# Where the softmax sums are divided out: spread by TensorE over the heads' outputs, or multiplied into the exponentials on ScalarE

## The chip, the core and the metric

The kernel runs on one core of a Trainium2 chip. Its metric is the device time of one execution in microseconds (us), median of three runs. Five engines take their instructions each from a queue of its own and in order: TensorE (PE, with its weight loads listed apart as PEld), VectorE (DVE), ScalarE (ACT), GpSimd (POOL) and SyncE (SP, which issues most DMAs). They meet at semaphores.

## The reference

A trunk of two layers over 512 frames of width 1024. Layer 0 has latent attention with 8 heads of 128 value features, layer 1 chunked attention with 16 heads of 64 features and a relative bias. A SwiGLU block follows each. What matters here is the softmax of both mixers:

```python
p = jax.nn.softmax(s, axis=-1).astype(v.dtype)        # layer 0
return jnp.einsum('bhqk,bkhd->bqhd', p, v)
...
p = jax.nn.softmax(s, axis=-1).astype(v_band.dtype)   # layer 1
o = jnp.einsum('bnhqk,bnkhd->bnqhd', p, v_band).reshape(B, S, B_HEADS * B_HEAD_DIM)
```

Each row of exponentials has to be divided by its sum. That can be done to the exponentials before the product with v, or to the product.

## The kernel before

All products are in fp32 split into a high and a low part, so that a product takes two or three passes of TensorE. `split` makes the parts: ACT casts the high one (L141), DVE subtracts it for the low one (L142).

A head is worked off in four slots, one for each block `qt` of 128 queries. Slot `qt` has `n = 128 * (qt + 1)` keys, so its tiles are 128, 256, 384 and 512 wide. `Head.scores` computes the scores on PE into a bank `sc` (L889 to L893 in layer 0, L1181 and L1182 in layer 1), then DVE adds mask or bias, takes the row minimum and writes the tile `p` (L396), and ACT makes the exponentials in place and adds up each row into one column of `sums` (L398, with a short second instruction that reads the accumulator). `Head.turn` has PE transpose `p` in blocks of 128x128 into a bank `pt` (L410), and splits the bank into `pth` and `ptl`. `pv` multiplies these with the values (L258 to L260 in layer 0, L1189 and L1190 in layer 1).

The products come out with features on the partitions and queries along the row, but `sums` has queries on the partitions. So the reciprocals have to be spread. In layer 0, `pv` takes the reciprocals of a head's four columns on DVE (L903), ACT copies the product out of its bank into `of` (L905), `spread` has PE transpose each column, broadcast to 128x128, into a bank `bc` (four transposes, L371), and DVE multiplies `of` by it (L908). In layer 1 two heads share the tile `of`: once for such a pair DVE takes the reciprocals (L1198), ACT writes them out as a tile `rw` in two copies (L1201), PE transposes that in four blocks into a bank `rs` (L1210), and DVE multiplies (L1211). Either way `of` is then split into `oh` and `ol`, the operands of the output projection.

`attention` runs the slots. While slot i is scored, slot i - 2 is turned; a head's `pv` follows six slots after its first. Between them `weave` puts steps of a filler: the projections of later heads, which need split weights (`whi`, `wlo`), and in the end the first output projections. The order on every engine is fixed when the program is built, by a list scheduler that goes by priorities and its own estimates of durations; on the chip each engine then keeps to that order. Banks are few: two for scores (tag `s`), two for transposes (tag `t`), four for products.

Of the kernel before, what the change touches and what calls it, by code (L numbers as in the profile page):

```python
# [11 lines left out]
F32R = mybir.dt.float32r  # L12
I32 = mybir.dt.int32
AF = mybir.ActivationFunctionType
OP = mybir.AluOpType
# [3 lines left out]
D, S, P = 1024, 512, 128  # L19
# [4 lines left out]
H_B, HD = 16, 64  # L24
# [6 lines left out]
NQT = S // P  # L31
# [37 lines left out]
def trunk(ctx: ExitStack, tc: tile.TileContext, a, out):  # L69
    nc = tc.nc  # L70
    V = nc.vector
# [10 lines left out]
    def name_(n):  # L82
        uid[0] += 1
        return f"{n}_{uid[0]}"

    def U(dt=F32, name="u"):
        return up.tile([P, S], dt, tag="u", name=name_(name), bufs=NU)
# [4 lines left out]
    def bank(tag="mm", name="b"):  # L92
        return ps.tile([P, S], F32, tag=tag, name=name_(name), bufs={"mm": 4, "s": 2, "t": 2}[tag])

    def small(name="sm"):
        return sp.tile([P, 4], F32, tag="small", name=name_(name))
# [17 lines left out]
    ident = consts.tile([P, P], F32, name="ident")  # L114
# [25 lines left out]
    def split(dst_hi, dst_lo, src):  # L140
        return (nc.scalar.copy(dst_hi, src),  # L141
                V.tensor_tensor(dst_lo, src, dst_hi.bitcast(F32), op=OP.subtract))  # L142
# [119 lines left out]
    def proj(n_out, n_k, kc, rhs, banks, ahead=True):  # L262

        cols = n_out * P
        for c in range(0, n_k, kc):
            m = min(kc, n_k - c)
            w = feed.next(m * cols, ahead)
            for kk in range(m):
                if kk == 1:
                    feed.ahead()  # L270
                while len(rhs) <= c + kk:
                    yield False
                for j in range(n_out):
                    mm3(banks[j], w(kk * cols + j * P, P), rhs[c + kk], c + kk == 0, c + kk == n_k - 1)
                    yield True
# [91 lines left out]
    def spread(col, first=0):  # L367

        b = bank("t", "bc")
        for i in range(col.shape[1]):  # L370
            nc.tensor.transpose(b[:, (first + i) * P:(first + i + 1) * P],  # L371
                                col[:, i:i + 1].to_broadcast([P, P]), ident)
        return b
# [8 lines left out]
    class Head:  # L382
# [7 lines left out]
        def scores(self, qt):  # L390
# [8 lines left out]
                                 accum_out=self.sums[:, qt:qt + 1])  # L399
            self.p[qt] = p  # L400

        def turn(self, qt):
            if self.pt is None:
                self.pt = [pool[0].tile([P, NQT, S], F32R, tag=t, name=name_(t), bufs=n)
                           for t, n in (("pth", 2), ("ptl", 1))]
            n = P * (qt + 1)
            p = self.p.pop(qt)
            t = bank("t", "pt")
            for kt in range(qt + 1):
                nc.tensor.transpose(t[:, kt * P:(kt + 1) * P], p[:, kt * P:(kt + 1) * P], ident)  # L410
            tv = t[:, :n].rearrange("p (a b) -> p a b", b=P)
            q_ = slice(qt * P, (qt + 1) * P)
            split(self.pt[0][:, :qt + 1, q_], self.pt[1][:, :qt + 1, q_], tv)

    def attention(n_heads, start, fill, first, units, after):


        slots = n_heads * NQT
        heads, done, late = {}, [0], []
        rate = (units - first) / slots  # L420

        def weave(upto):
            n = 0
            while (n < 4 if fill.scored else done[0] < upto) and fill.step():
                done[0] += 1
                n += 1

        for i in range(slots + 3):
            h, qt = divmod(i, NQT)
            if h < n_heads:  # L430
                if qt == 0:
                    heads[h] = start(h)
                    if h == 0:
                        weave(first)
                heads[h].scores(qt)
                fill.scored = i == slots - 1
            weave(first + rate * (i + 0.5))
            if late and not after:
                late.pop()()
            if i >= 6 and i % NQT == 2:  # L440
                t = heads.pop((i - 6) // NQT)
                late.append(t.pv(*t.pt))
            if 2 <= i < slots + 2:
                t, qt = divmod(i - 2, NQT)
                heads[t].turn(qt)
            if late and i % NQT == 3:
                late.pop()()
            weave(first + rate * (i + 1))
        if late:
            late.pop()()  # L450
# [231 lines left out]
    rest = proj(3, KT, 2, xs, b2)  # L682
# [4 lines left out]
    for j in range(2):  # L687
        t = U(name="ckv")
# [79 lines left out]
    qr, qk_a, osp = {}, {}, []  # L768
# [113 lines left out]
    def start_a(h):  # L882
        fill.until(h)
        qh, ql, kh, kl = qk_a.pop(h)
        r = qr.pop(h)

        def qk(o, qt, n):
            q_ = slice(qt * P, (qt + 1) * P)
            nc.tensor.matmul(o, qh[:, q_], kh[:, :n], start=True, stop=False)  # L889
            nc.tensor.matmul(o, qh[:, q_], kl[:, :n], start=False, stop=False)  # L890
            nc.tensor.matmul(o, ql[:, q_], kh[:, :n], start=False, stop=False)
            nc.tensor.matmul(o, r[:, q_], kr1[:, :n], start=False, stop=False)
            nc.tensor.matmul(o, r[:, q_], kr2[:, :n], start=False, stop=True)  # L893

        def pv(pth, ptl):
            fill.until("v")
            o = bank()
            v_ = slice(h * VD, (h + 1) * VD)
            for kt in range(NQT):
                q_ = slice(kt * P, S)  # L900
                mm3(o[:, q_], (va[kt][:, 0, v_], va[kt][:, 1, v_]), (pth[:, kt, q_], ptl[:, kt, q_]),
                    kt == 0, kt == NQT - 1)
            V.reciprocal(sums, sums)  # L903
            of = U(name="of")
            nc.scalar.copy(of, o)  # L905

            def rest():
                V.tensor_tensor(of, of, spread(sums), op=OP.mult)  # L908
                oh, ol = U(F32R, "oh"), U(F32R, "ol")
                split(oh, ol, of)  # L910
                osp.append((oh, ol))

            return rest

        sums = small("sums")
        return Head(qk, lambda n: mask[:, S - n:], lambda qt: nsq[:, qt:qt + 1], pv, sums)

    firsts = []
# [201 lines left out]
    rest = v_half(0)  # L1120
# [13 lines left out]
    osp, qk_b, ofs, sums, biases = [], {}, {}, {}, {}  # L1134
# [34 lines left out]
    def start_b(h):  # L1169
        pr, e = divmod(h, 2)  # L1170
        fill.until(pr)
        q1, k1, k2 = qk_b[pr]
        bt = biases.pop(h)
        if h + 1 < H_B:
            bias(h + 1)
        if e == 0:
            sums[pr] = sp.tile([P, 2, NQT], F32, tag="sums", name=f"sums_{pr}", bufs=3)

        def qk(o, qt, n):
            q_ = slice(qt * P, (qt + 1) * P)  # L1180
            nc.tensor.matmul(o, q1[:, e, q_], k1[:, e, :n], start=True, stop=False)  # L1181
            nc.tensor.matmul(o, q1[:, e, q_], k2[:, e, :n], start=False, stop=True)  # L1182

        def pv(pth, ptl):
            o = bank()
            for kt in range(NQT):
                q_ = slice(kt * P, S)
                vv = vb[kt][:, h].rearrange("p a d -> p (a d)")
                nc.tensor.matmul(o[:, q_], vv, pth[:, kt, q_], start=kt == 0, stop=False)  # L1189
                nc.tensor.matmul(o[:, q_], vv, ptl[:, kt, q_], start=False, stop=kt == NQT - 1)  # L1190
            if e == 0:
                ofs[pr] = U(name="of")
            of = ofs[pr]
            t = U(name="ot")
            nc.scalar.copy(t[:64], o[64:])
            V.tensor_tensor(of[(LO, HI)[e]], o[:64], t[:64], op=OP.add)
            if e:
                V.reciprocal(sums[pr], sums[pr])  # L1198
                rw = U(name="rw")
                for j in range(2):  # L1200
                    nc.scalar.copy(rw.rearrange("p (i e d) -> p i e d", e=2, d=HD)[:, :, j],  # L1201
                                   sums[pr][:, j].unsqueeze(2).to_broadcast([P, NQT, HD]))

            def rest():
                if e == 0:
                    return
                r = bank("t", "rs")
                for i in range(NQT):
                    i_ = slice(i * P, (i + 1) * P)
                    nc.tensor.transpose(r[:, i_], rw[:, i_], ident)  # L1210
                V.tensor_tensor(of, of, r, op=OP.mult)  # L1211
                oh, ol = U(F32R, "oh"), U(F32R, "ol")
                split(oh, ol, of)
                osp.append((oh, ol))

            return rest

        return Head(qk, lambda n: bt[:, :n][:, ::-1], lambda qt: -1.0, pv, sums[pr][:, e])

    bias(0)  # L1220
# [119 lines left out]
```

## Time and profile before

| | |
|---|---|
| median of 3 runs | 1162.41 us (1161.83 to 1162.87) |
| the profiled execution's own time | 1162.01 us |
| its span, first to last instruction | 1159.9 us |
| granted TensorE clock, mean | 0.997 |
| PE, PEld busy | 1137.9 us, 1018.7 us |
| DVE, ACT busy | 828.8 us, 613.9 us |

The span leaves out 2.1 us of the profiled execution's time, at its start and end. Busy times are shares of the whole span; matmuls are pipelined and overlap in the profile, so that a busy PE need not be a PE at its peak. Layer 0's heads lie at about 64 to 166 us of the span, layer 1's at about 609 to 770 us.

### The profile page before, as it was taken

To read this page: it belongs to the slowest core of one execution; us is meant where nothing else is said; L and a number is where in the kernel's file an instruction comes from. 1 tells how busy PE (TensorE), PEld (TensorE's weight loads), DVE (VectorE), ACT (ScalarE), POOL (GpSimd) and SP (SyncE) were. 2 spreads that over 40 slices of the span, in tenths; PEclk is the share of its full clock that TensorE was granted. 3 is DMA by queue.
4 is the path that set the end of the run, shared out by engine and by line. 5 is a ranking of instruction groups with operands and counts; after the bars stand their busy time and mean duration, and the time that the engine had idled before them with its cause. 6 is when DMAs were issued, how large, how long until landed. Compare 5 with 4: busy or idle time off the path is not lost.

```text
span 1159.9 us, 18693 instructions
## 1 busy us (share of the span) xinstructions
PE 1137.9 (98%) x7195; PEld 1018.7 (88%) x7195; DVE 828.8 (71%) x1429; ACT 613.9 (53%) x1159; POOL 29.5 (3%) x51
## 2 busy tenths in 40 slices
PE   9999999999999999999999999999999999999996
PEld 6788889899999998889788887789899999998886
DVE  7787648999898862246968877748998998852233
ACT  6476646656565542224436766656655565632220
POOL 1200000000000000000100000000000000000002
PEclk9999999999999999999999999999999999999998
DMA  7333144323333253233456656454223233252212
GB/s 231 117 113 91 37 149 160 109 79 105 109 92 127 74 170 103 96 118 96 159 158 159 172 152 164 128 176 138 87 92 114 90 108 109 73 189 89 91 50 73
DMA packets 53161, 137.71 MB, mean 119 GB/s; under 512 B 7184, under 2 KB 10768, under 8 KB 53072
## 3 DMA queue, kind: packets, MB, share of 16 engines
q1 hardware_dynamic: 52928, 136.47, 37.6%
q8 instruction: 57, 0.93, 0.3%
q14 instruction: 32, 0.26, 0.1%
q10 hardware_dynamic: 144, 0.04, 0.0%
HBM read 113.22 MB, written 8.59 MB: 105 GB/s over the span
## 4 chain that ended last, share of the span: by engine, by line
PE 85%; DVE 7%; ACT 3%; issue 2%; DMA 2%; POOL 1%; SPq 0%; DVEq 0%; ACTq 0%; POOLq 0%
PE al L1064 16%; PE b L258 16%; PE b L259 16%; PE b L260 16%; PE be L1064 8%; PE ga L1064 4%; PE pt L410 2%; DVE wlo L142 1%; DVE acc L328 1%; POOL r L354 1%; DMA raw<-in_w_pair 1%; ACT whi L141 1%; PE b L1189 1%; PE bc L371 1%; PE b L1190 1%
## 5 line engine op out<-in xcount | busy, mean ns | idle before, releaser
L142 DVE TENSOR_TENSOR wlo<-raw,whi 128x1024 fp32r<-128x1024 f32 (+4 forms) x240 | 278.8, 1162 | 199.0 <-ACT whi L141 197.3
L141 ACT CAST whi<-raw 128x1024 fp32r<-128x1024 f32 (+4 forms) x240 | 240.7, 1003 | 337.8 <-PE b L259 180.6
L258 PE MATMUL b<-hh,whi 128*128 128x512 f32 (+1 forms) x364 | 136.0, 374 | 0.0
L259 PE MATMUL b<-hl,whi 128*128 128x512 f32 (+1 forms) x364 | 135.7, 373 | 0.0
L260 PE MATMUL b<-hh,wlo 128*128 128x512 f32 (+1 forms) x364 | 135.6, 373 | 0.0
L1064 PE MATMUL al<-th,whi 128*128 128x256 f32 x432 | 124.2, 288 | 0.6 <-DVE ut L1076 0.3
L1064 PE MATMUL al<-tl,whi 128*128 128x256 f32 x432 | 122.1, 283 | 0.0
L1064 PE MATMUL al<-th,wlo 128*128 128x256 f32 x432 | 122.1, 283 | 0.0
L258 PE MATMUL b<-xh,whi 128*128 128x512 f32 (+1 forms) x304 | 115.7, 383 | 0.8 <-ACT xh L145 0.8
L259 PE MATMUL b<-xl,whi 128*128 128x512 f32 (+1 forms) x304 | 113.1, 372 | 0.0
L260 PE MATMUL b<-xh,wlo 128*128 128x512 f32 (+1 forms) x304 | 112.8, 371 | 0.0
L171 DVE TENSOR_TENSOR raw<-raw,raw 128x1024 f32<-128x1024 f32 x72 | 86.6, 1218 | 1.1 <-DMA raw<-in_w_pair 0.9
L1064 PEld LDWEIGHTS al<-th,whi 128*128 128x128 f32 x432 | 82.7, 191 | 2.9 <-DVE ut L1076 0.8
L1064 PEld LDWEIGHTS al<-th,wlo 128*128 128x128 f32 x432 | 82.7, 192 | 0.0
L1064 PEld LDWEIGHTS al<-tl,whi 128*128 128x128 f32 x432 | 82.7, 191 | 0.0
L259 PEld LDWEIGHTS b<-hl,whi 128*128 128x128 f32 x364 | 68.5, 188 | 12.0
L258 PEld LDWEIGHTS b<-hh,whi 128*128 128x128 f32 x364 | 68.5, 188 | 12.0
L260 PEld LDWEIGHTS b<-hh,wlo 128*128 128x128 f32 x364 | 68.5, 188 | 11.9
L398 ACT ACTIVATE p<-p,mn 128x128 f32<-128x128 f32 (+1 forms) x96 | 54.0, 562 | 31.9 <-DVE mn L396 31.2
L142 DVE TENSOR_TENSOR ptl<-pt,pth 128x128 fp32r<-128x128 f32 (+1 forms) x96 | 46.3, 485 | 28.8 <-ACT pth L141 23.0
L328 DVE TENSOR_TENSOR acc<-acc,sq 128x256 f32<-128x256 f32 (+1 forms) x89 | 43.3, 505 | 32.1 <-ACT sq L327 31.3
L258 PEld LDWEIGHTS b<-xh,whi 128*128 128x128 f32 x304 | 57.4, 189 | 9.0 <-ACT xh L145 2.1
(266 smaller groups left out, 2831.0 us busy)
## 6 DMA issues: line engine op xcount, KB each, us to landing
raw<-in_w_pair SPq DMA_DIRECT2D x72, 512.0 KB, 3.8
raw<-in_w_down SPq DMA_DIRECT2D x38, 512.0 KB, 3.4
raw<-in_w_o SPq DMA_DIRECT2D x16, 512.0 KB, 3.6
raw<-in_w_gu SPq DMA_DIRECT2D x16, 512.0 KB, 3.7
raw<-in_w_qkb SPq DMA_DIRECT2D x16, 512.0 KB, 3.6
x<-in_x SPq DMA_DIRECT2D x16, 256.0 KB, 5.8
mid<-x SPq DMA_DIRECT2D x16, 256.0 KB, 2.2
x<-mid SPq DMA_DIRECT2D x16, 256.0 KB, 6.2
```

The costliest lines, as they stand in the source:

```text
L141: return (nc.scalar.copy(dst_hi, src), V.tensor_tensor(dst_lo, src, dst_hi.bitcast(F32), op=OP.subtract))
L142: V.tensor_tensor(dst_lo, src, dst_hi.bitcast(F32), op=OP.subtract))
L171: V.tensor_tensor(t, x, y, op=OP.add)
L258: nc.tensor.matmul(o, l[0], r[0], start=start, stop=False)
L259: nc.tensor.matmul(o, l[0], r[1], start=False, stop=False)
L260: nc.tensor.matmul(o, l[1], r[0], start=False, stop=stop)
L328: V.tensor_tensor(self.acc[:, c], self.acc[:, c], q[:, c], op=OP.add)
L354: nc.gpsimd.tensor_tensor(r, v, mhalf[:, :m], op=OP.pow)
L371: nc.tensor.transpose(b[:, (first + i) * P:(first + i + 1) * P], col[:, i:i + 1].to_broadcast([P, P]), ident)
L398: nc.scalar.activation(p[:, :n], p[:, :n], AF.Exp, bias=mn[:, :1], scale=-1.0, accum_out=self.sums[:, qt:qt + 1])
L410: nc.tensor.transpose(t[:, kt * P:(kt + 1) * P], p[:, kt * P:(kt + 1) * P], ident)
L1064: nc.tensor.matmul(o, l[c], r[d], start=first_ and n == 0, stop=k == K2 - 1 and n == 2, skip_group_check=True)
```

## The change

A new step `norm` stands between `scores` and `turn`, one slot behind the scores: DVE takes the reciprocal of one column of sums, and ACT multiplies the exponentials by it in place. What spread the reciprocals over the products goes, and so does the multiplication there. In layer 0 the split into `oh` and `ol` now reads the product's bank directly.

```diff
+        def norm(self, qt):
+            n = P * (qt + 1)
+            p = self.p[qt][:, :n]
+            V.reciprocal(self.sums[:, qt:qt + 1], self.sums[:, qt:qt + 1])
+            nc.scalar.activation(p, p, AF.Copy, scale=self.sums[:, qt:qt + 1])
+
         def turn(self, qt):
...
+            if 1 <= i < slots + 1:
+                t, qt = divmod(i - 1, NQT)
+                heads[t].norm(qt)
             weave(first + rate * (i + 0.5))
...
-            V.reciprocal(sums, sums)
-            of = U(name="of")
-            nc.scalar.copy(of, o)
-
-            def rest():
-                V.tensor_tensor(of, of, spread(sums), op=OP.mult)
-                oh, ol = U(F32R, "oh"), U(F32R, "ol")
-                split(oh, ol, of)
-                osp.append((oh, ol))
-
-            return rest
+            oh, ol = U(F32R, "oh"), U(F32R, "ol")
+            split(oh, ol, o)
+            return lambda: osp.append((oh, ol))
...
-            if e:
-                V.reciprocal(sums[pr], sums[pr])
-                rw = U(name="rw")
-                for j in range(2):
-                    nc.scalar.copy(rw.rearrange("p (i e d) -> p i e d", e=2, d=HD)[:, :, j],
-                                   sums[pr][:, j].unsqueeze(2).to_broadcast([P, NQT, HD]))
 
             def rest():
                 if e == 0:
                     return
-                r = bank("t", "rs")
-                for i in range(NQT):
-                    i_ = slice(i * P, (i + 1) * P)
-                    nc.tensor.transpose(r[:, i_], rw[:, i_], ident)
-                V.tensor_tensor(of, of, r, op=OP.mult)
                 oh, ol = U(F32R, "oh"), U(F32R, "ol")
```

The scheduler orders the changed program anew, so other instructions move as well. Three places show how. A number behind a name tells tiles of one name apart, and lines from `norm` on are shifted.

The first place is PE's queue at the end of layer 0's fourth head: the transposes of its last slots (`pt`), a projection (`b<-ck...`) and the first matmul with the transposed exponentials (`b<-pth`). Before:

```order
L410 MATMUL pt_1304<-ident,p_1237 128x128 x4
L258 MATMUL b_1317<-ckh_444,whi_1192 128x512
L259 MATMUL b_1317<-ckl_445,whi_1192 128x512
L260 MATMUL b_1317<-ckh_444,wlo_1193 128x512
L258 MATMUL b_1317<-ckh_449,whi_1192 128x512
L259 MATMUL b_1317<-ckl_450,whi_1192 128x512
L260 MATMUL b_1317<-ckh_449,wlo_1193 128x512
L258 MATMUL b_1331<-pth_1215,va_530 128x512
```

And of the changed kernel:

```order
L258 MATMUL b_1324<-ckh_444,whi_1202 128x512
L259 MATMUL b_1324<-ckl_445,whi_1202 128x512
L260 MATMUL b_1324<-ckh_444,wlo_1203 128x512
L258 MATMUL b_1324<-ckh_449,whi_1202 128x512
L259 MATMUL b_1324<-ckl_450,whi_1202 128x512
L260 MATMUL b_1324<-ckh_449,wlo_1203 128x512
L416 MATMUL pt_1281<-ident,p_1194 128x128 x3
L416 MATMUL pt_1311<-ident,p_1248 128x128 x4
L258 MATMUL b_1340<-pth_1226,va_530 128x512
```

The projection that stood between the last transposes and the first matmul on `pth` now stands ahead of the transposes.

The second place is PE's queue at the start of layer 1's last pair of heads, from the last score matmul of the pair's first slot (`sc`, 128 wide) to that slot's transpose (`pt`). Before:

```order
L1182 MATMUL sc_8055<-k_7_7826,q_7_7824 128x128
L1182 MATMUL sc_8076<-k_7_7826,q_7_7824 128x256
L259 MATMUL b_8063<-ol_7682,whi_8085 128x512
L260 MATMUL b_8063<-oh_7681,wlo_8086 128x512
L258 MATMUL b_8062<-oh_7920,whi_8085 128x512
L259 MATMUL b_8062<-ol_7921,whi_8085 128x512
L1181 MATMUL sc_8102<-k_7_7825,q_7_7824 128x384
L1182 MATMUL sc_8102<-k_7_7826,q_7_7824 128x384
L1181 MATMUL sc_8137<-k_7_7825,q_7_7824 128x512
L410 MATMUL pt_8130<-ident,p_8058 128x128
```

And of the changed kernel:

```order
L1183 MATMUL sc_8097<-k_7_7864,q_7_7862 128x128
L1183 MATMUL sc_8120<-k_7_7864,q_7_7862 128x256
L1191 MATMUL b_8160<-ptl_8049,vb_5881 128x128
L260 MATMUL b_8106<-oh_7954,wlo_8132 128x512
L1182 MATMUL sc_8148<-k_7_7863,q_7_7862 128x384
L1183 MATMUL sc_8148<-k_7_7864,q_7_7862 128x384
L1182 MATMUL sc_8181<-k_7_7863,q_7_7862 128x512
L1183 MATMUL sc_8181<-k_7_7864,q_7_7862 128x512
L258 MATMUL b_8107<-oh_7954,whi_8131 128x512
L259 MATMUL b_8107<-ol_7955,whi_8131 128x512
L416 MATMUL pt_8174<-ident,p_8100 128x128
```

Between a slot's scores and its transpose there is about the same PE work as before, and the slot's exponentials now pass through one more engine step on the way.

The third place is ACT's queue in layer 1's seventh and eighth heads, from the exponentials of the seventh head's last slot (128x512) on. Before:

```order
L398 ACTIVATE p_7097,sums_6892<-p_7097,mn_7098 128x512
L141 CAST pth_7088<-pt_7133 128x3x128
L398 ACTIVATE p_7126,sums_7122<-p_7126,mn_7127 128x128
L141 CAST pth_7088<-pt_7152 128x4x128
L398 ACTIVATE p_7145,sums_7122<-p_7145,mn_7146 128x256
L141 CAST whi_7375<-raw_7109 128x1024
L398 ACTIVATE p_7165,sums_7122<-p_7165,mn_7166 128x384
L141 CAST fh_7170<-f_7169 128x512
```

And of the changed kernel:

```order
L398 ACTIVATE p_7113,sums_6904<-p_7113,mn_7114 128x512
L398 ACTIVATE p_7144,sums_7140<-p_7144,mn_7145 128x128
L398 ACTIVATE p_7165,sums_7140<-p_7165,mn_7166 128x256
L398 ACTIVATE p_7187,sums_7140<-p_7187,mn_7188 128x384
L141 CAST fh_7194<-f_7193 128x512
L406 ACTIVATE p_7113<-p_7113,sums_6904 128x512
L406 ACTIVATE p_7144<-p_7144,sums_7140 128x128
L406 ACTIVATE p_7165<-p_7165,sums_7140 128x256
L406 ACTIVATE p_7187<-p_7187,sums_7140 128x384
L141 CAST pth_7104<-pt_7174 128x4x128
```

The four scalings (L406) stand between the exponentials and the cast of the transposed tile, which was two places behind its exponentials and is now nine behind.

## Rows read from the trace of the kernel before

**Rows 1.** The page's first part: busy us (share of the span) xinstructions.

```profile
PE 1137.9 (98%) x7195; PEld 1018.7 (88%) x7195; DVE 828.8 (71%) x1429; ACT 613.9 (53%) x1159; POOL 29.5 (3%) x51
```

**Rows 2.** Windows: stretch, length, busy us of PE, PEld, DVE, ACT, POOL, clock, DMA.

```profile
64.00:166.00 102.00, 101.37 (x581) 87.26 (x580) 67.64 (x156) 59.88 (x143) 0.00 (x0) 1.00 0.25 77
609.00:681.00 72.00, 71.81 (x394) 59.85 (x393) 61.19 (x143) 51.13 (x127) 1.02 (x7) 1.00 0.63 165
681.00:770.00 89.00, 86.14 (x458) 68.92 (x458) 57.31 (x138) 54.46 (x135) 0.87 (x6) 1.00 0.50 128
```

**Rows 3.** Timeline of PE: start us, us, engine, line, operation; x4 merges four.

```profile
738.16 0.39 PE L260 MATMUL b<-oh,wlo 128*128 128x512 f32 x1
738.39 0.63 PE L410 MATMUL pt<-ident,p 128*128 128x128 f32 x4
738.77 0.47 PE L258 MATMUL b<-oh,whi 128*128 128x512 f32 x1
739.08 0.39 PE L259 MATMUL b<-ol,whi 128*128 128x512 f32 x1
```

**Rows 4.** Tiles bc and rs: the spreading transposes, ns min/median/max, starts.

```profile
L371 PE MATMUL bc<-ident,sums x32: 270/273/291, 80.7 to 163.9; 128*128 128x128 f32 x32
L1210 PE MATMUL rs<-ident,rw x32: 270/273/330, 632.2 to 769.6; 128*128 128x128 f32 x32
```

**Rows 5.** Waits in 609 to 770: engine, line, waited for; us, times, longest.

```profile
PE rs L1210 <- ACT rw L1201: 0.6, 2, 0.4
PE rs L1210 <- DVE ptl L142: 0.3, 1, 0.3
...
PEld rs L1210 <- ACT rw L1201: 1.5, 3, 0.6
...
PEld rs L1210 <- issue: 0.6, 1, 0.6
PEld rs L1210 <- DVE ptl L142: 0.5, 1, 0.5
```

**Rows 6.** Groups of ACT by form: busy us, mean ns of one, idle before.

```profile
L398 ACT ACTIVATE p<-p,mn 128x512 f32<-128x512 f32 x24 | 17.4, 726 | 9.9 <-DVE mn L396 9.8
L398 ACT ACTIVATE p<-p,mn 128x384 f32<-128x384 f32 x24 | 14.8, 615 | 3.8 <-DVE mn L396 3.7
L141 ACT CAST pth<-pt 128x512 fp32r<-128x512 f32 x24 | 14.1, 585 | 7.8 <-PE pt L410 7.5
L398 ACT ACTIVATE p<-p,mn 128x256 f32<-128x256 f32 x24 | 12.2, 507 | 4.1 <-DVE mn L396 3.8 <-ACT p L398 0.2
L398 ACT ACTIVATE p<-p,mn 128x128 f32<-128x128 f32 x24 | 9.6, 402 | 14.1 <-DVE mn L396 13.8
L1201 ACT COPY rw<-sums 128x256 f32<-128x256 f32 x16 | 5.6, 400 | 0.0
L1020 ACT ACTIVATE xg<-x,gains 128x512 f32<-128x512 f32 x8 | 5.5, 715 | 0.0
L905 ACT COPY of<-b 128x512 f32<-128x512 f32 x8 | 4.7, 585 | 5.7 <-PE b L260 5.7
```

**Rows 7.** Groups of DVE by form, same columns.

```profile
L908 DVE TENSOR_TENSOR of<-of,bc 128x512 f32<-128x512 f32 x8 | 5.5, 683 | 3.0 <-ACT of L905 2.6 <-PE bc L371 0.4
L1211 DVE TENSOR_TENSOR of<-of,rs 128x512 f32<-128x512 f32 x8 | 5.5, 682 | 1.3 <-PE rs L1210 1.3
L903 DVE RECIPROCAL sums<-sums 128x4 f32<-128x4 f32 x8 | 1.4, 176 | 1.2 <-ACT p L398 0.9
```

**Rows 8.** Timeline of one slot of layer 1, 256 wide.

```profile
611.13 0.28 PE L1182 MATMUL sc<-k,q 128*128 128x256 f32 x1
...
611.45 0.42 DVE L396 CUSTOM_DVE_ANT_0 p<-sc,bias 128x256 f32<-128x256 f32 x1 [0.47 <-PE sc L1182]
...
611.91 0.51 ACT L398 ACTIVATE p<-p,mn 128x256 f32<-128x256 f32 x1 [0.41 <-DVE mn L396]
...
612.33 0.19 ACT L398 ACTIVATION_READ_ACCUMULATOR p<-p,mn 128x1 f32 x1
```

## The prediction

> **What bounds the kernel now.** I read the page's busy shares first, then windows over the two stretches that the change touches, then PE's waits there. PE is busy for 98% of the span and no other engine for more than 71% [rows 1]. In layer 0's heads PE is busy for 101.4 of 102 us, in the first half of layer 1's heads for 71.8 of 72, in the second half for 86.1 of 89; ACT is busy there for 59.9, 51.1 and 54.5 us, DVE for 67.6, 61.2 and 57.3 [rows 2]. The granted clock is 1.00 in all three, so the clock has nothing to give. A PE that is nearly always busy sets these stretches as long as its transfers and operands come in time, so work taken from PE should shorten them, and work given to ACT should be free until ACT is late. What the reader is to watch is the second row: there DVE (85%) and ACT (71%) have the least to spare.
>
> **What is removed from PE.** Eight spreads in layer 0 and eight in layer 1, of four transposes each: 64 [rows 4]. One lasts 273 ns, but they overlap. What a group costs is read from start to start: a 512-wide matmul starts 0.23 us before its successor (738.16 to 738.39); from the first of four transposes to the second matmul behind them it is 0.69 us (738.39 to 739.08), so the group adds 0.69 - 0.23 = 0.46 us [rows 3]. 16 x 0.46 = 7.4 us. From below it is the 0.38 us to the next start, 6.1 us in all.
>
> The Trainium skill prices this otherwise: TensorE: Matmul & The Clock Gate, PE-mode transpose, puts one such transpose at about 275 ns inside a kernel. The trace's 273 ns agree as a duration, but by that price the 64 would be 17.6 us and the time 1144; the start-to-start spacing of four in 0.38 us contradicts it as a cost, and the measurement decides.
>
> With the spreads of layer 1 go the waits ahead of them: PE stood 0.9 us for `rw` and `ptl` ahead of `rs`, its weight loads 2.6 us [rows 5]. A running matmul hides a part of the second figure; I take 1.8 us, between the two. Layer 0 shows no such waits.
>
> **What is removed elsewhere.** ACT loses eight copies of 0.585 us in layer 0 and sixteen of 0.40 us in layer 1, DVE sixteen multiplications of 0.68 us and sixteen reciprocals of about 0.18 us [rows 6, 7]. That shortens the way from a head's product to `oh`, for which PE has other work.
>
> **What is added.** Per slot one reciprocal of a single column on DVE, which the trace lacks; the nearest is the one of four columns, 176 ns, bounded below by nothing and above by that [rows 7]. And one scaling on ACT: no row has it for all widths; the same operation 512 wide took 715 ns, the exponentials, which also read a column per partition, 402, 507, 615 and 726 ns by width [rows 6]. I take the exponentials' durations: 2.25 us per head. For ACT that makes:
> - layer 0: 8 x 2.25 - 8 x 0.585 = 13.3 us more, 73.2 of 102 us, 72%;
> - layer 1, first half: 8 x 2.25 - 8 x 0.40 = 14.8 us more, 65.9 of 72 us, 92%;
> - second half: again 14.8 us, 69.3 of 89 us, 78%.
>
> For DVE, 32 reciprocals less four of the old and four multiplications make 2.2 us more in layer 1's first half, 63.4 of 72 us; in layer 0 it is 1.3 us less.
>
> The chain from scores to transposed tile grows by the reciprocal, the scaling and two handovers. A 256-wide slot took from the start of its last score matmul (611.13) to the end of the exponentials (612.42) 1.29 us, and to the end of the accumulator's read 1.39 us; each handover in it is some 0.04 us [rows 8]. With 0.18 and 0.51 us and three handovers behind the read it becomes 2.2 us, 0.9 more; for 128 wide about 2.0, for 512 about 3.1.
>
> **What covers the longer chain.** PE's own work between a slot's scores and its transposes. Counted over the two orders, at 0.23 us per 512 columns and 0.1 us per transpose, it is on average 5.8 us in layer 0 before and after, and 4.3 us before against 5.3 us after in layer 1: the new order moves the transposes back by about what the chain grows. So most slots cost nothing; without that cover each would cost 0.9 us, 86 us for all 96. Three kinds of places are not covered.
> - Four heads have less between their last transposes and the first matmul on `pth` than the cast of the transposed tile takes. The first order quoted is the worst: six matmuls, 1.4 us, before; none now. The transposes run on for 0.63 us, of which 0.38 pass before the next start [rows 3], and the cast takes 0.585 [rows 6], so PE stands about 0.9 us. Three heads of layer 1 have 0.2 to 0.45 us left of 0.9 to 1.7: 0.7, 0.5 and 0.4 us. Together 2.5 us. What is late behind it is that head's whole product, and then its `oh`.
> - Pairs of layer 1's second half start with little filler. In the second order quoted 3840 columns, 1.7 us, stand from the first slot's score matmul to its transpose against a need of 2.0; the third and fourth slots of that pair miss some 0.7 us more. With two other pairs at 0.2 us: 1.3 us.
> - ACT's queue in layer 1's first half. In the third order quoted a cast that PE's products need stands behind four scalings, 2.25 us. The scaling waits for DVE's reciprocal, and exponentials, casts and weight parts (`whi`) queue behind it; a weight part late by that stops the filler. From below it costs nothing, from above 10 us (worked out under the rivals). I take 1.5 us, near the lower end, because ACT was idle for 20.9 of 72 us and two score banks and two transpose banks let PE run ahead by a slot.
>
> One edit I cost at nothing: in layer 0 the product's bank is now held until DVE's subtraction, some 0.7 us longer. Four product banks rotate, which hides it; without them it would be up to 8 x 0.7 = 5.6 us.
>
> **The sum.** -7.4 - 1.8 + 2.5 + 1.3 + 1.5 = -3.9 us. Against the profiled execution's 1162.0 us that is 1158.1; the median of the runs is 0.4 us above it, so 1158.4 us.
>
> **The rivals.**
> - *ACT becomes the bound of layer 1's first half; slower.* ACT has 65.9 us of work there. An engine that takes its queue in order also keeps part of its waits, since DVE's minimum and PE's transposes still come when they come: before, 20.9 us. The other terms of the sum leave -5.4 us, and the stretch's own share of the gain, some 2 us, is lost when ACT sets its length. If three quarters of the waits stay (15.7 us), the stretch is 81.6 us, 9.6 more, and the time 1162.4 - 3.4 + 9.6 = 1168.6. It turns the sign once more than about 72 + 3.4 - 65.9 = 9.5 us of the 20.9 stay. For it: 92%, DVE at 88%, and a new round trip between the two in each slot. Against it: waits shrink when an engine falls behind.
> - *PE was not the bound, the removed work is hidden anyway; no change.* Then the stretches keep their length, because DVE and ACT in turn hand PE its operands at the pace they have, and the time is 1162. For it speaks only DVE's 85%. Against it: in PE's queue a 512-wide matmul follows every 0.23 us [rows 3], and PE stands for little. The Trainium skill has a rule that points this way: Perfetto Trace Analysis, Identifying the Most-Contended Engine, says that matmul busy time is a poor measure of TensorE's headroom and that weight-load busy time is a better one. That is 59.9 of 72 us here, 83%, which would leave 12 us of room for the removed groups and put the time at 1162; but the back-to-back spacing shows a full PE at such a share, so the trace agrees with the first half of the rule more than with the second. The same time results if the three uncovered places cost 9.2 us in place of 5.3.
> - *Everything is covered; faster by the whole.* -9.2 us, 1153.2. For it: the mean distances above. Against it: the first order quoted, where nothing is left to cover.
>
> **How the numbers follow.** No change can be told from a difference under about 0.2%, 2.3 us. The forecast at 1158.4 with its own range of 1154 to 1160 has 0.44, the full gain 0.10: faster 0.54. No change has 0.20. ACT as the bound has 0.21, and the uncovered product bank or a mixture past it 0.05: slower 0.26. The range runs from the full gain, 1153.2, to the price of the ACT rival, 1168; outside it I leave some 0.05 below and 0.1 above.
>
> **What the profile would show.** Right: no `bc<-ident,sums` and no `rs` rows; PE busy about 6 to 7 us less; ACT busy about 43 us more (18 + 36 us of scalings less 11 of copies); layer 0's heads some 3 us shorter; PE waits on the casts of `pth` and on scaled `p` of a few us in layer 1. Wrong: PE's waits on ACT in the first half of layer 1 of 8 us or more, with ACT busy above 90%, would be the first rival; stretches of unchanged length with longer PE idle spread over all slots would be the second. The prediction would also fail if a scaling took clearly more than an exponential, or the one-column reciprocal much more than 0.18 us, since there are 96 of each.

## The result, and the profile after

The changed kernel takes 1164.5 us, the kernel before 1162.45 (medians of ten runs each): ratio 1.0019, 95% interval 1.0010 to 1.0028. The forecast of 1158.4 had the wrong sign. The loss stands in layer 1's heads and not in layer 0's, as four stretches show. They are read from PE's timeline, from and to the start of a matmul: layer 0's heads (first score to last PV), the first half of layer 1's heads (first score to the ninth head's first score), the second half (to the last PV), and from there to the gated FFN's first product. "Second profile" is the changed kernel run again, word for word. Each row is one profiled execution (1162.0, 1166.6 and 1163.6 us), so a stretch carries its scatter: the two of the changed kernel differ by 1.4 us in the first half.

| us | layer 0 | layer 1, first half | second half | to the products |
|---|---|---|---|---|
| before | 99.2 | 71.3 | 86.9 | 77.0 |
| after | 97.9 | 78.9 | 87.5 | 74.8 |
| after, second profile | 97.9 | 77.5 | 87.4 | 74.8 |

The page's busy line, for [rows 1], and windows of the changed kernel, for [rows 2]:

```profile
PE 1136.6 (98%) x7131; PEld 1012.0 (87%) x7131; DVE 827.1 (71%) x1493; ACT 644.6 (55%) x1231; POOL 29.5 (3%) x51
```

```profile
64.00:166.00 102.00, 100.31 (x552) 84.87 (x551) 66.60 (x175) 70.53 (x169) 0.00 (x0) 1.00 0.26 79
609.00:681.00 72.00, 67.77 (x345) 53.39 (x344) 57.17 (x156) 57.26 (x144) 1.02 (x7) 0.98 0.61 156
670.00:680.00 10.00, 7.64 (x36) 5.47 (x36) 7.24 (x21) 7.19 (x19) 0.14 (x1) 0.90 0.52 154
680.00:690.00 10.00, 9.30 (x47) 7.79 (x46) 5.58 (x12) 5.59 (x10) 0.00 (x0) 0.93 0.42 94
681.00:770.00 89.00, 85.77 (x436) 66.64 (x435) 60.15 (x168) 66.66 (x161) 0.87 (x6) 1.00 0.48 125
```

The page alone misleads: PE is 98% busy as before and 1.3 us less in sum. The second window shows the change: PE is idle for 4.2 of 72 us (before 0.2), and yet ACT is busy for only 57.3, DVE for 57.2. No engine is full there, and the granted clock is below 1.00.

The added operations, by form (line, engine, busy us, mean ns of one, idle before it):

```profile
L406 ACT ACTIVATE p<-p,sums 128x512 f32<-128x512 f32 x24 | 17.3, 722 | 1.4 <-DVE sums L405 1.4
L405 DVE RECIPROCAL sums<-sums 128x1 f32<-128x1 f32 x96 | 14.8, 158 | 13.0 <-ACT p L398 12.5
L406 ACT ACTIVATE p<-p,sums 128x128 f32<-128x128 f32 x24 | 9.4, 393 | 0.2 <-DVE sums L405 0.2
```

They last what the forecast gave them, and no row of the spreading transposes [rows 4] is left. What waits in 605 to 690 us (engine, line, waited for: us, times, longest), for [rows 5]:

```profile
DVE ptl L142 <- PE b L1191: 7.4, 4, 2.9
...
PEld pt L416 <- ACT p L406: 3.0, 10, 0.4
DVE raw L222 <- DMA raw<-in_w_qkb: 2.9, 3, 1.8
PEld sc L1182 <- DVE mn L396: 2.9, 3, 2.1
...
PEld b L1190 <- ACT pth L141: 2.8, 7, 0.9
...
PE sc L1182 <- DVE mn L396: 2.0, 2, 1.8
...
PE pt L416 <- DVE ptl L142: 1.6, 2, 1.4
```

The first row did not exist before (7.1 us in 4 in the second profile): DVE's subtraction for `ptl` waits for a PV product (L1191). PV is short for the product with the values. `ptl` has one buffer, so the next head's first part can't be written until PE has done the PV that reads the last head's. How this closes into a ring is seen in one slot, 512 wide, from its last score matmul to its transposes:

```profile
665.97 0.39 PE L1183 MATMUL sc<-k,q 128*128 128x512 f32 x1
...
669.02 1.23 DVE L222 TENSOR_TENSOR raw<-raw,gains 128x1024 f32<-128x1024 f32 x1 [0.62 <-DMA raw<-in_w_qkb]
...
670.17 0.68 DVE L142 TENSOR_TENSOR ptl<-pt,pth 128x512 fp32r<-128x512 f32 x1
...
670.91 0.51 PE L1191 MATMUL b<-ptl,vb 128*128 128x512 f32 x1
...
672.21 0.58 ACT L1196 COPY ot<-b 64x512 f32<-64x512 f32 x1 [2.28 <-PE b L1191]
672.26 0.29 DVE L142 TENSOR_TENSOR ptl<-pt,pth 128x128 fp32r<-128x128 f32 x1 [1.41 <-PE b L1191]
672.47 0.68 DVE L396 CUSTOM_DVE_ANT_0 p<-sc,bias 128x512 f32<-128x512 f32 x1
...
673.57 0.72 ACT L398 ACTIVATE p<-p,mn 128x512 f32<-128x512 f32 x1
...
674.80 1.04 ACT L141 CAST whi<-raw 128x1024 fp32r<-128x1024 f32 x1
...
675.74 0.72 ACT L406 ACTIVATE p<-p,sums 128x512 f32<-128x512 f32 x1
...
675.88 0.44 PE L1182 MATMUL sc<-k,q 128*128 128x384 f32 x1 [1.79 <-DVE mn L396]
...
676.57 0.60 PE L416 MATMUL pt<-ident,p 128*128 128x128 f32 x4
```

The score is done at about 666.4. DVE reduces it only at 672.47. Of these 6.1 us its queue has some 4.1 us of other work ahead of the reduction, waits 0.6 us for a weight, and stands 1.41 us because `ptl` waits for PV. The scaled `p` ends at 676.46, 10.5 us after the score began; a weight cast of 1.04 us stands ahead of the scaling in ACT's queue. In the meantime the score banks are full and PE stands for 1.79 us.

### The profile page after: what moved, and what is told of

Same layout as the page of the kernel before. It is cut to its first block, busy times and chain, and to the rows that moved or that the text cites. A ratio compares the mean times of both kernels' runs of the same rounds, so it can differ in the third digit from the quotient of the medians.

```text
span 1164.8 us, 18691 instructions
## 1 busy us (share of the span) xinstructions
PE 1136.6 (98%) x7131; PEld 1012.0 (87%) x7131; DVE 827.1 (71%) x1493; ACT 644.6 (55%) x1231; POOL 29.5 (3%) x51
## 4 chain that ended last, share of the span: by engine, by line
PE 81%; DVE 7%; ACT 5%; DMA 3%; issue 2%; POOL 1%; SPq 0%; DVEq 0%; ACTq 0%; POOLq 0%
PE al L1065 17%; PE b L258 15%; PE b L259 15%; PE b L260 15%; PE be L1065 8%; PE ga L1065 4%; PE pt L416 2%; DMA raw<-in_w_qkb 1%; DVE wlo L142 1%; DVE acc L328 1%; ACT whi L141 1%; ACT p L398 1%; POOL r L354 1%; DMA raw<-in_w_pair 1%; PE b L1190 1%
## 5 line engine op out<-in xcount | busy, mean ns | idle before, releaser
L1065 PEld LDWEIGHTS al<-th,whi 128*128 128x128 f32 x432 | 82.7, 191 | 2.1 <-DVE ut L1077 0.3
L1065 PEld LDWEIGHTS al<-tl,whi 128*128 128x128 f32 x432 | 82.7, 191 | 0.0
L258 PEld LDWEIGHTS b<-xh,whi 128*128 128x128 f32 x304 | 57.7, 190 | 10.5 <-ACT xh L145 3.2
```

The source lines that it names most:

```text
L258: nc.tensor.matmul(o, l[0], r[0], start=start, stop=False)
L1065: nc.tensor.matmul(o, l[c], r[d], start=first_ and n == 0, stop=k == K2 - 1 and n == 2, skip_group_check=True)
```

## The experiments

Times are medians. Each ratio is to runs of the kernel before that were taken beside it (1162.1 to 1162.3 us) and has a 95% interval; a stretch is read from one profiled execution. Line numbers shift by a few lines where an edit adds some. Four theories of the loss are told apart. Theory 1: the new round trip between ACT and DVE in each slot. Theory 2, the load: ACT's added time itself. Theory 3: weights that come late because SP's queue is held by a late `fh`. The last, named the way theory: the whole way from a score to its scaled `p`, with the queues in it, no longer fits in the two slots that it has.

**One layer at a time.** The edit keeps the old code in the other layer:

```
-                heads[t].norm(qt)
+                if n_heads == H_A:       # layer 0; H_B for layer 1
+                    heads[t].norm(qt)
```

Expected of layer 0 alone: 

> Scaling of the exponentials in layer 0 alone; layer 1 is as before. Theory 1 (the loss is a round trip: DVE's reciprocal stands in its queue until ACT's exponentials are done, ACT's scaling stands until the reciprocal is done, and both keep other work waiting; it costs where ACT and DVE are both full, which is layer 1's first half): layer 0 keeps the 1.3 us that the profiles show there (99.2 to 97.9 us from its first scores to its last product), so about 1161 us against 1162.4. Theory 2 (the loss is ACT's added work as such): the same sign, as ACT has room in layer 0, 1159 to 1161. If it comes out at 1163 or above, the loss is not confined to layer 1.

Expected of layer 1 alone: 

> Scaling of the exponentials in layer 1 alone; layer 0 is as before. Both theories: slower than before by the whole loss and without layer 0's gain, 1165 to 1167 us against 1162.4; the stretch from layer 1's first scores to the first scores of its ninth head some 5 to 8 us longer than before (71.3 us). If it comes out at 1162 or below, the place is wrong.

Layer 0 alone: 1160.3 us, 0.9982 (0.9973 to 0.9991). Layer 1 alone: 1165.75 us, 1.0027 (1.0016 to 1.0037). By the medians layer 0 gains 1.8 us and layer 1 loses 3.7; together that is the loss of the whole change.

**Half of the addition.** The changed kernel without the reciprocals (it multiplies by the sums and leaves the division out), and the kernel before with scalings on ACT whose results, in bfloat16, nobody reads:

```
-            V.reciprocal(self.sums[:, qt:qt + 1], self.sums[:, qt:qt + 1])
```
```
+            nc.scalar.activation(junk[:, :n], p, AF.Copy, scale=ones)
```

Expected without reciprocals: 

> The changed kernel without its 96 reciprocals: the exponentials are multiplied by their sums instead of divided (the output is not the reference's). ACT's work is the same, but ACT no longer waits for DVE between exponentials and scaling, and DVE no longer waits for ACT's exponentials in 96 more places. Theory 1: most of what PE was spared comes through, 1156 to 1159 us, DVE's 13.0 us of waits ahead of the reciprocals are gone and PE's weight loads wait less than half of 12.1 us for the scaled tile. Theory 2: ACT is as full as it was, 1163 to 1165 us.

Expected of the idle scalings: 

> The kernel before, with 96 more ACT instructions of the sizes of the scalings in the same places of the program: they read the exponentials, multiply them by one and write them to a tile that nobody reads (in bfloat16, for room). ACT gets about 54 us more work and nobody waits for its result. Theory 1: little happens, 1162 to 1164 us. Theory 2: ACT is late in layer 1's first half, 1166 to 1170 us.

Without reciprocals 1162.05 us, 1.0003 (0.9993 to 1.0013); idle scalings 1170.0 us, 1.0062 (1.0048 to 1.0076). This looked like ACT's load: the idle scalings lost 8 us with no round trip at all, and the run without reciprocals came out between what theory 1 and theory 2 gave. The stretches warn against reading it so. Of the idle scalings' loss only 2.5 us stood in layer 1's first half (73.8), 4.5 in the second (91.4), 0.9 in layer 0. Without the reciprocals the first half takes 72.1 us, 5.4 to 6.8 less than in the changed kernel, so that most of the loss there hangs on them; layer 0 (99.5) and the second half (89.3) are longer and hide it in the sum. In layer 0 that goes with the clock, 0.98 in the first of these windows where the changed kernel has 1.00:

```profile
64.00:166.00 102.00, 99.89 (x545) 85.24 (x544) 61.51 (x140) 70.38 (x167) 0.00 (x0) 0.98 0.25 76
609.00:681.00 72.00, 70.82 (x378) 57.31 (x377) 58.18 (x135) 61.62 (x153) 1.02 (x7) 1.00 0.64 164
```

**Nothing added.** The step between scores and transposes taken out, so that nothing divides by the sums:

```
-            if 1 <= i < slots + 1:
-                t, qt = divmod(i - 1, NQT)
-                heads[t].norm(qt)
```

Expected: 

> The changed kernel without its reciprocals and scalings: nothing divides by the sums any more (the division is left out), and nothing is put on VectorE or ScalarE in its place. What is left of the change is what it removes. Forecast's terms: -7.4 us of transposes and multiplies, -1.8 us of waits for rs, and +1.3 us for less filler in layer 1, so 1154 to 1155 us. If the removed transposes were covered and not worth their price, the run gives 1158 to 1160 us, and then the changed kernel's additions cost only 5 to 6 us and not 9 to 10.

1152.9 us, 0.9923 (0.9909 to 0.9936): what the change removes is worth 9.3 us, and what it adds costs some 11.6 (1164.5 less 1152.9, from different groups of runs). Its windows, with PE full in the first half:

```profile
609.00:681.00 72.00, 71.75 (x391) 59.73 (x390) 58.89 (x137) 49.54 (x121) 1.01 (x7) 1.00 0.68 170
681.00:770.00 89.00, 87.21 (x468) 71.80 (x467) 56.69 (x134) 54.51 (x132) 0.87 (x6) 1.00 0.54 144
```

Its first half takes 69.8 us, its second 82.7. So the additions cost 7.7 to 9.1 us in the first half (two profiles) and 4.7 to 4.8 in the second.

**Late weights.** In the changed kernel SP's queue held transfers of q and k for a late `fh` for 21.5 us in 605 to 690 us (8.5 before), and weight loads stood behind them. A third theory made that the start of the loss. Loads one group further ahead, and the q and k transfers on another queue:

```
-                self.load(j + 2)
+                self.load(j + 2 + self.deep)     # deep = 1 in layer 1's heads
```
```
-                        nc.sync.dma_start(d[rows, e].bitcast(F32), src[own])
+                        nc.gpsimd.dma_start(d[rows, e].bitcast(F32), src[own])
```

Expected of the first: 

> The changed kernel, with each weight load of layer 1's heads issued one group further ahead. Theory 3 (the late ScalarE holds fh, the q and k transfers wait for fh at the head of SP's queue, the weight load behind them is issued late, VectorE stands for it with ptl behind it, TensorE stands for ptl): VectorE's waits on in_w_qkb (2.9 us) and TensorE's 1.4 us on ptl go, and with them the half clock behind a stand; the time falls by 2 to 5 us to 1159.5 to 1162.5. Theory 2 (ScalarE's added time holds p and pth back by itself): the weight element goes but the time stays within 1 us of 1164.5, and the waits for p stay near 12 us.

Expected of the second: 

> The changed kernel, with the q and k transfers of layer 1 issued from GpSimd's queue in place of SP's, so that a late fh no longer holds the weight loads and the biases. Theory 3: SP's waits on fh (21.5 us) leave SP, weights come early, the time falls by 2 to 5 us to 1159.5 to 1162.5. Theory 2: within 1 us of 1164.5. A third outcome: the transfers themselves start later behind the bias fills of GpSimd's queue, scores wait for q and k, and the run is over 1165.5 us.

1165.5 us, 1.0025 (1.0016 to 1.0033), and 1180.1 us, 1.0147 (1.0130 to 1.0164). The waits in 605 to 690 us of the first, then of the second:

```profile
DVE raw L223 <- DMA raw<-in_w_qkb: 3.0, 2, 2.2
```

```profile
DVE raw L222 <- DMA raw<-in_w_qkb: 5.7, 5, 2.2
...
PE sc L1183 <- DMA k<-f: 3.0, 2, 2.8
```

Neither edit brought the weights sooner (before: no such wait; after: 2.9 us), and the second made q and k late. The theory was not tested by them; the next runs settle it otherwise.

**A slot more of distance.** The transposes three slots behind the scores, in place of two:

```
-            if 2 <= i < slots + 2:
-                t, qt = divmod(i - 2, NQT)
+            if 3 <= i < slots + 3:
+                t, qt = divmod(i - 3, NQT)
                 heads[t].turn(qt)
...
```

(PV and its rest move along by a slot.)

Expected: 

> The changed kernel with every head's transposes one slot later behind its scores (three slots in place of two). If TensorE's 12.1 us of waits for p come from the length of the chain from score to scaled p (exp, reciprocal, scaling: latency), they fall under 4 us and the time falls by 3 us or more, to at most 1161.5. If ScalarE is simply short of time in layer 1's first half, a slot more only moves the wait to exp, pth or fh, and the time stays within 1.5 us of 1164.5.

1164.5 us, 1.0019 (1.0009 to 1.0029), no change, but by two opposite effects: the first half of layer 1 fell from 78.9 to 69.1 us, less than before; layer 0 rose to 102.0 and the second half to 92.4 (granted clock 0.98 in 64 to 166 us and 0.96 in 690 to 780). So three slots were given to a part alone, with `j + lag(j) == i` in place of `j + 2 == i` for the transposes, and PV and its rest moved along:

```
+        def lag(j):
+            return 3 if after and j < 33 else 2      # after: layer 1
```

(57 in place of 33 for the second run, all of layer 1 for the third, and 33 in the kernel before for the fourth.)

Expected of 33: 

> The changed kernel with the transposes three slots behind the scores in the first 33 slots of layer 1 alone (two everywhere else, as before). The way theory (the scaling costs because the way from a score to its scaled p no longer fits in two slots of about 2.2 us when VectorE's and ScalarE's queues are in it): layer 1's first half takes at most 71 us (78.9 in the changed kernel, 69.1 in the run with three slots everywhere) and the second half stays at 87 to 88, so 1155 to 1158 us, faster than both kernels. The load theory (ScalarE has no time left in that half): 1163 to 1166 us.

Expected of 57: 

> As the run before, with three slots for the first 57 slots of layer 1. The way theory: the second half's waits for p (TensorE's weight loads 7.0 us in 19 there) go as well, 1 to 3 us below the run with 33 slots, 1153 to 1157. If in the second half other waits bind (pth for PV, q and k), no better than with 33 slots, within 1 us of it.

Expected of all: 

> Three slots in the whole of layer 1, two in layer 0. Against the run with three slots everywhere (1164.5 us; layer 0's heads took 102.0 us there in place of 97.9): 4 us less, about 1160.5, if its loss in layer 0 is real; and 1 to 5 us above the run with 57 slots, if the loss of its second half (92.4 us in place of 87.5) comes from the end, where the last transposes and PVs have no other work between them and the clock falls.

Expected of the control: 

> Control: the kernel before with the same three slots in the first 33 slots of layer 1. The way theory: its way has no scaling in it, its waits for p there were under 2 us in all, so it gains at most 2 us: 1160 to 1162.5. If the greater distance is worth as much without the scaling, it falls to 1152 to 1156, and the distance says nothing of the change.

| | us | ratio (95%) | layer 0 | first half | second half |
|---|---|---|---|---|---|
| first 33 slots | 1157.2 | 0.9953 (0.9940 to 0.9965) | 97.8 | 69.0 | 88.3 |
| first 57 slots | 1161.1 | 0.9987 (0.9978 to 0.9996) | 97.9 | 69.1 | 92.5 |
| all of layer 1 | 1162.0 | 0.9996 (0.9988 to 1.0005) | 97.8 | 69.4 | 92.3 |
| before, first 33 | 1162.0 | 0.9996 (0.9987 to 1.0005) | 99.1 | 71.3 | 87.8 |

With three slots in the first half the change beats both kernels, and the distance by itself is worth nothing to the kernel before. Carried on to 57 slots or to all of layer 1 it gave less than expected: the second half grows by 4 us. The window of the run with 33 slots, to set beside the changed kernel's:

```profile
609.00:681.00 72.00, 71.39 (x382) 58.71 (x381) 61.72 (x174) 63.64 (x160) 1.01 (x7) 1.00 0.65 164
```

ACT does more in the same 72 us than in the changed kernel (63.6 for 57.3) and PE is full. Its time was not short there. In 605 to 690 us DVE's wait on the weights is down to 0.2 us, PE's on `ptl` to 0.3 and `ptl`'s on PV to 1.8 (before the extra slot 2.9, 1.6 and 7.4), though SP's q and k transfers still stood 8.3 us for `fh` and 16.6 for scalings. So late weights look like a link of the ring and not its start; no run took them out by themselves.

**Against the idle scalings, and a second profile.** The same distance in the kernel with idle scalings and in the one without reciprocals, and the changed kernel once more:

Expected: 

> The kernel before, with the 96 scalings on ScalarE whose results nobody reads (1170.0 us with two slots, 8 us slower than before), and the transposes three slots behind the scores in layer 1's first 33 slots. Nobody waits for these scalings; they stand in ScalarE's queue ahead of the next exp and of pth. The way theory: there too the time was lost because exps and pth came later than two slots allow; with three slots layer 1's first half (73.8 us in the run with two) falls to at most 71, and the time to 1164 to 1167. The load theory: ScalarE's time is lost whatever the distance, 1169 to 1171 us.

Expected: 

> The changed kernel with three slots in layer 1's first 33 slots and without the 96 reciprocals (p is multiplied by the sums, so the division is left out). With two slots the reciprocals cost 2.5 us (1162.05 in place of 1164.5). The way theory: with three slots the first half no longer feels them, and at most 1.5 us are left, 1155.7 to 1157.2 us against 1157.2. If VectorE's 14.8 us of reciprocals cost by its load, again 2 to 3 us: 1154 to 1155.

Expected: 

> The changed kernel once more, word for word, for a second profile and as a control of the spread: 1163.5 to 1165.5 us. If the half clock behind TensorE's stand at about 675 us belongs to the change it is there again, with layer 1's first half near 78.9 us; if it was that execution's alone, the half takes about 77 us and TensorE stands for less than 1.5 us at a time.

Idle scalings 1172.0 us, 1.0087 (1.0075 to 1.0099); without reciprocals 1161.9 us, 0.9998 (0.9990 to 1.0007); the changed kernel again 1164.4 us, 1.0019 (1.0010 to 1.0028). The first two lie above what either theory gave. The first half fell by 1.5 and 2.0 us, to 72.3 and 70.1, but the second halves are 93.7 and 90.4 us; what is lost there the distance doesn't give back. In the first half the reciprocals now cost nothing, 69.0 us with them and 70.1 without, so DVE's added work as such was not the loss.

The end of layer 1's heads shows one reason. When the last scores are issued, PE has few projections left. Windows of 5 us, of the changed kernel, of the run with 57 slots, and of the idle scalings with 33:

```profile
755.00:760.00 5.00, 3.58 (x18) 2.60 (x19) 3.49 (x13) 4.98 (x15) 0.00 (x0) 1.00 0.01 2
```

```profile
745.00:750.00 5.00, 2.96 (x12) 1.89 (x12) 2.87 (x14) 4.77 (x14) 0.00 (x0) 0.79 0.29 104
750.00:755.00 5.00, 5.00 (x18) 4.07 (x17) 2.79 (x8) 3.14 (x10) 0.00 (x0) 0.53 0.00 0
```

```profile
750.00:755.00 5.00, 2.92 (x15) 1.97 (x13) 2.28 (x8) 4.95 (x17) 0.00 (x0) 0.89 0.38 119
755.00:760.00 5.00, 4.22 (x16) 3.69 (x16) 3.48 (x10) 3.05 (x7) 0.00 (x0) 0.50 0.00 0
```

Here ACT is full (4.8 to 5.0 of 5 us) and PE stands for 1.4 to 2.1 us. In the changed kernel it stands for scaled `p` (PE's timeline):

```profile
755.12 0.44 PE L416 MATMUL pt<-ident,p 128*128 128x128 f32 x2 [0.41 <-ACT p L406]
756.62 0.55 PE L416 MATMUL pt<-ident,p 128*128 128x128 f32 x3 [1.07 <-ACT p L406]
```

In this one place the scalings do cost ACT's time. In the other two runs shown, the granted clock falls there. In the run with 57 slots the two windows lose (1 - 0.79) x 5 + (1 - 0.53) x 5 = 3.4 us to it, an estimate that takes PE to set the pace. That is most of what its second half has over that of the run with 33 slots (92.5 for 88.3), whose clock is 1.00 in 690 to 780 us. Over the same 90 us the clock is 0.96 with idle scalings, with either distance, 0.98 with three slots in all of layer 1 and without reciprocals at three slots, and 1.00 in both kernels.

## Why the prediction was wrong

**What is removed: right in sum, not in place.** The forecast had -7.4 and -1.8 us; without anything added the kernel is 9.3 us faster. In its profile 0.3 us stood in layer 0's heads, where 3.7 were forecast, 1.5 and 4.2 in layer 1's halves, and 1.4 behind the heads. The profiled execution was 1.7 us above the median, and a granted clock of 0.83 in 105 to 115 us (1.00 before) took about as much of layer 0's part, an estimate from 0.17 x 10. So the sum fits the group price read from start to start, but no run took out the groups alone, and that it fits so closely is partly luck. The Trainium skill's 275 ns for a PE-mode transpose (TensorE: Matmul & The Clock Gate, PE-mode transpose) agrees with its duration, 273 ns [rows 4]; 64 times that, 17.6 us, did not come as a gain. The Trainium skill's advice to judge TensorE's headroom by weight-load busy time, beside MFU, the matmul work done as a share of the peak (Perfetto Trace Analysis, Identifying the Most-Contended Engine), is not borne out as the second rival used it: weight loads were busy for 83% of the first half [rows 2], and yet that half became 1.5 us shorter.

**What is added: the operations right.** Scalings of 393 to 722 ns against 402 to 726 taken; reciprocals 158 ns against a bound of 176. They sum to the 54 us forecast. ACT's busy time rose by only 30.7 us in place of 43, since rows of neighbouring instructions overlap in it; their durations added up rose by 41.9. PE's fell by 1.3 us, where 6 to 7 were forecast.

**The uncovered place of layer 0: right in kind.** At the first order quoted PE's weight load waited 1.4 us for 0.9 forecast; the row of the changed kernel's waits in 64 to 166 us:

```profile
PEld b L258 <- ACT pth L141: 1.4, 1, 1.4
```

Layer 0's heads became 1.3 us shorter, and not 2.8; the gain of the removed groups is what fell short there.

**The step that failed: "What covers the longer chain".** It read the chain from one slot in which every engine was free [rows 8], 1.39 us and 2.2 with the scaling, and set 5.3 us of PE's work against it, so that most slots would cost nothing. Over all 32 slots of layer 1's first half, from the start of the last score matmul (means from the timelines):

| us after the score | unscaled `p` ends | scaled `p` ends | transposes start |
|---|---|---|---|
| before | 2.9 | | 5.1 |
| nothing added | 2.8 | | 5.0 |
| no reciprocals | 3.1 | 4.3 | 5.3 |
| no reciprocals, three slots | 3.0 | 4.1 | 7.3 |
| three slots, 33 | 3.0 | 5.1 | 7.2 |
| after | 4.5 | 6.3 | 7.2 |

With the queues in it the chain is 2.9 us long before and, where nothing holds it up, 5.1 with the scaling: the addition is 2.2 us and not 0.9, because the reciprocal starts 0.8 us behind the accumulator's read and the scaling 0.5 behind the reciprocal (run with 33 slots), each with other work ahead of it in its queue. The cover was sized well, 5.3 us for 5.0 to 5.1; it was the chain that was taken too short. It then ends when the transposes are due at two slots. The last row is what follows: one late `p` makes `pth` late, so PV, so DVE behind the one `ptl` buffer, so the next reductions (2.8 us after the score in place of 1.6), and all ways grow to 6.3 us. With three slots the cover is 7.2 us against 5.1, and the loss is gone; without the reciprocals the chain is 4.3 us, fits into two slots, and most of the loss is gone too (72.1 us). These two, with the control, show that the chain's length against its distance is the cause in this half. How the delay spreads by way of `ptl` is read from the trace: no run gave `ptl` a second buffer.

**The term "ACT's queue in layer 1's first half": mis-sized.** It stood at 1.5 us with bounds of 0 and 10; it is 7.7 to 9.1, near the upper end. The reason given for the lower end, that PE can run ahead by a slot on two score and two transpose banks, left out that DVE takes its queue in order and `ptl` has one buffer: the score banks were full, and PE stood 1.79 us for one. In the third order quoted ahead of the forecast, the cast was three places behind its exponentials before the change, not two.

**The rival of the ACT bound: half right.** It had the place, the sign and "a new round trip between the two in each slot". Its mechanism, ACT setting the stretch's length at 92%, is refuted there: at 88% (63.6 of 72 us) with three slots PE is full, and in the changed kernel ACT was busy for 80%, not above 90%. It holds for about 5 us at the end of the heads. The round trip over the reciprocal is a part of the chain's length: 2.5 us of the whole kernel (1162.05 against 1164.5), 5.4 to 6.8 of the first half with two slots, and nothing there with three.

**"Pairs of layer 1's second half": too small.** 1.3 us forecast, 4.7 to 4.8 measured. The end of the heads, where ACT is full, holds a part of it; the weight loads' waits for scaled `p`, 7.0 us in 681 to 770 (2.0 for unscaled `p` before), the rest at most. How the two share stays open; leaving out the reciprocals did not shorten this half (89.3 us). It differs by up to 7 us (86.9 to 93.7) between kernels that leave its order almost alone. Of that some 3.6 us goes with the clock (0.96 in place of 1.00 over 90 us); the rest stays open.

## What to carry to other kernels

Read the length of a chain of engines as a mean over many slots under load, and set it against the distance at which it is consumed; one free slot gave it too short by half (1.3 us for 2.9). A step that is put into such a chain may need the consumer one stage later, and that only where there is work to fill the stage: three slots in the first half gained 7.3 us, and 4 of them were lost again when they were kept on to near the end. Before stretches of two kernels are compared, set their granted clocks side by side. Before believing that PE can run ahead, count the single buffers whose release goes through PE itself.

## What the runs showed of the hardware

PE's clock fell after short stands. In both profiles of the changed kernel PE stood for 1.8 us near 672 to 676 us, and a little later its 512-wide matmuls started 0.43 us apart in place of 0.23, for some 3.5 us, with a granted clock of 0.90 and 0.83 in that window. The first profile:

```profile
677.87 0.74 PE L1190 MATMUL b<-pth,vb 128*128 128x512 f32 x1 [0.46 <-ACT pth L141]
...
679.47 0.63 PE L260 MATMUL b<-xh,wlo 128*128 128x512 f32 x1
679.90 0.63 PE L1191 MATMUL b<-ptl,vb 128*128 128x512 f32 x1
680.32 0.52 PE L1190 MATMUL b<-pth,vb 128*128 128x384 f32 x1
...
682.04 0.39 PE L259 MATMUL b<-xl,whi 128*128 128x512 f32 x1
682.27 0.39 PE L260 MATMUL b<-xh,wlo 128*128 128x512 f32 x1
```

The second:

```profile
670.00:680.00 10.00, 7.83 (x36) 5.84 (x35) 6.80 (x21) 8.37 (x21) 0.15 (x1) 0.83 0.37 107
```

That is the lower of its two levels, 1.2 in place of 2.4 GHz: a stand of 1.8 us cost about as much again, an estimate from 3.5 us at half the pace. The kernel before shows 1.00 in all windows of its heads, and with three slots in the first half it is 1.00 again. At 755 to 760 us PE stood for 1.4 us in all in the changed kernel, 1.07 at a time, without a fall. With layer 1 alone changed it stood there just so, for 0.42 and 1.07 us, and the clock did fall (0.98 in 690 to 780 us). So such stands sometimes bring a fall and sometimes none.
